# Deeper row buffers, a reordered product and an earlier convolution in a two-layer diffusion backbone

## The chip, the cores and the metric

The kernel runs on one core of a Trainium2 chip. The metric is the time of one execution in microseconds (us) on the device. Below, PE is the matrix engine, DVE the vector engine, ACT the scalar engine, POOL the GpSimd engine, and SP the engine that issues most loads. DMA transfers of all of them share 16 DMA engines.

## The reference

Two layers over 512 latent tokens x and 256 context tokens, width 1024, all in float32. A layer is a set of token mixers and then a PEER expert network:

```python
p = xn @ wl                                   # one input projection, 10 blocks of 1024 columns
attn = attn_out_norm(blocked_diff_attn(q, k, v, lam))
conv = (b_gate * depthwise_conv(c_gate * h, conv_w)) @ conv_out_w
merged = g[0] * attn + g[1] * pool + g[2] * conv      # g = sigmoid of three blocks of p
h = h + mod[2] * (merged @ w_out)

q = (xc @ w_q).reshape(T, 8, 2, 128)          # PEER: 8 heads, two halves
s = einsum('thid,hikd->thik', q, sub_keys)    # 128 keys per half; top 16 of each, top 16 of their sums
u = u_emb[eidx]                               # 128 of 16384 experts per token
hid = gelu(einsum('td,thkd->thk', xc, u))
h = h + mod[5] * einsum('thk,thkd->td', gate * hid, v_emb[eidx])
```

The context runs through the first layer completely; in the second it gives only keys and values.

## The kernel before

Weights and activations are split into a high and a low float32r part (`split`, lines 91 to 94: ACT copies the high part, DVE subtracts it to get the low one), and each product is three matmuls (`mm3`, lines 96 to 100): high by high, low by high, high by low. A weight tile is loaded by SP, split by ACT, then by DVE, and only then can PE use its low part.

The PEER network is computed in two ways. *Gathered*: for 256 context tokens in layer 0 and the last 128 x tokens in layer 1, the chosen rows of `peer_u` and `peer_v` are fetched, 128 tokens by 1024 floats a time, by an indirect DMA that POOL issues (line 855), into a buffer named `row`; DVE multiplies each with the token (line 868) or adds it to a sum (line 878). That makes 256 fetches for each 128 tokens, 768 in all: 512 in layer 0, 256 in layer 1. *Dense*: for 512 x tokens in layer 0 and 384 in layer 1 all 16384 experts are computed. `hidden` (line 766) loads 128 tiles `uraw`, splits each into `uh` and `ul`, and forms 128 products `hid` of 24 matmuls. `values` (line 817) forms 128 products `dps` in each layer from `vraw` tiles (`vh`, `vl`), added by DVE into `acc` (lines 838, 840). In layer 1 the first 20 of 32 chunks have their hidden parts stored, and the last 12 alternate between `hidden` and `values` (lines 1134 to 1140).

The gathered work is written at a priority 40000 steps behind, so it is meant to fill gaps of the dense work that runs beside it. A scheduler simulates the whole program and writes a fixed order of instructions for every engine; each engine then executes its own list strictly in that order. So if DVE's next instruction is a row that has not landed, everything behind it on DVE waits, splits included.

In layer 0 the order of stages is: attention of both streams, the context's mixers (`"pcgo"`), x's pooling, then `ctx_ffn` (norm, `keys`, `pick`, and the start of the gathered work of 256 tokens), x's remaining mixers (`mixers`, letters: g attention's gate, c convolution, o convolution's output and `w_out`), x's dense network with its own keys, `hidden`, `values`. `mm` tiles of x's mixers are taken from a pool of 3 PSUM banks (line 972), of which a core has 8. `hss` and `hrb` are the small matmuls of attention's gate (lines 492, 502, 503); `rsc` are the scores of `keys`; `gps` builds the gates of the dense experts.

Of the kernel before, what the change touches and what calls it, by code (L numbers as in the profile page):

```python
# [21 lines left out]
F32 = mybir.dt.float32  # L22
# [8 lines left out]
PSUM = bass.MemoryType.PSUM  # L31

P = 128
D = 1024
KT = D // P
# [34 lines left out]
class Net:  # L70
# [695 lines left out]
    def hidden(self, l, y, up, uq, cs, ahead, keep=False):  # L766

        nc, a = self.nc, self.a
        tiles = []
        for c in cs:  # L770
            if l:
                ge = up.tile([P, 4, y.n], F32, name="ge", bufs=1 + self.EC)
                tiles.append(ge)
            for e in range(4):
                with self.prio(-ahead):
                    raw = up.tile([P, KT, P], F32, name="uraw", bufs=3)
                    nc.sync.dma_start(raw.rearrange("p k e -> p (k e)"), a["uT"][l, 4 * c + e])
                    uh = up.tile([P, KT, P], F32R, name="uh", bufs=2)
                    ul = up.tile([P, KT, P], F32R, name="ul", bufs=2)
                    self.split(uh, ul, raw)  # L780
                hid = uq.tile([P, y.n], F32, name="hid", bufs=3)
                for k in range(KT):
                    self.mm3(hid, uh[:, k], ul[:, k], y.h[:, k], y.l[:, k], k == 0, k == KT - 1)
                with self.prio(-ahead):
                    g = ge[:, e] if l else up.tile([P, y.n], F32, name="ge", bufs=4)
                    nc.scalar.activation(g, hid, AF.Gelu_apprx_tanh)
                    if not l:
                        nc.scalar.dma_start(self.hidd[c][:, e * y.n:(e + 1) * y.n], g)
            if l and not keep:
                with self.prio(-ahead):  # L790
                    nc.scalar.dma_start(self.hidd[c][:, :4 * y.n], ge.rearrange("p e t -> p (e t)"))
        return tiles
# [56 lines left out]
    def gathered(self, l, tiles, gp, gq, nat, late):  # L849

        nc, a = self.nc, self.a

        def fetch(t, idx, s):
            r = gp.tile([P, D], F32, tag="row", name="row", bufs=3)
            nc.gpsimd.indirect_dma_start(out=r, out_offset=None, in_=a[t],  # L855
                                         in_offset=bass.IndirectOffsetOnAxis(ap=idx[:, s:s + 1], axis=0))
            return r

        for row, idx, g, hsrc, i, dst in tiles:
            with self.prio(late):  # L860
                x = gp.tile([P, D], F32, name="gx", bufs=1)
                nc.sync.dma_start(x, nat[row:row + P, :])
                acc = gp.tile([P, D], F32, name="gacc", bufs=1)
                for h in range(8):
                    hid = gp.tile([P, 16], F32, name="ghid", bufs=2)
                    for k in range(16):
                        r = fetch("peer_u", idx, h * 16 + k)
                        nc.vector.scalar_tensor_tensor(out=r, in0=r, scalar=1.0, in1=x, op0=OP.mult, op1=OP.mult,  # L868
                                                       accum_out=hid[:, k:k + 1])
                    w = gp.tile([P, 16], F32, name="gw", bufs=2)  # L870
                    nc.scalar.activation(w, hid, AF.Gelu_apprx_tanh)
                    nc.vector.tensor_tensor(w, w, g[:, h * 16:h * 16 + 16], op=OP.mult)
                    for k in range(16):
                        r = fetch("peer_v", idx, h * 16 + k)
                        if h == 0 and k == 0:
                            nc.vector.tensor_scalar(acc, r, w[:, k:k + 1], None, op0=OP.mult)
                        else:
                            nc.vector.scalar_tensor_tensor(acc, r, w[:, k:k + 1], acc, op0=OP.mult, op1=OP.add)  # L878
            res = gp.tile([P, KT, P], F32, tag="row", name="gres", bufs=3)
            nc.sync.dma_start(res, hsrc.rearrange("(k p) t -> p k t", p=P))  # L880
            tr = gq.tile([P, 4, P], F32, tag="gtr", name="gtr", bufs=1)
            for k in range(KT):
                nc.tensor.transpose(tr[:, k % 4], acc[:, k * P:(k + 1) * P], self.ident)
                nc.vector.scalar_tensor_tensor(res[:, k], tr[:, k % 4], self.modT[l][:, 40 + k, i:i + 1], res[:, k], op0=OP.mult, op1=OP.add)
            nc.sync.dma_start(dst.rearrange("(k p) t -> p k t", p=P), res)
# [10 lines left out]
    def run(self):  # L896
        nc, tc, a = self.nc, self.tc, self.a
        dt = lambda name, shape=(D, NT): tc.dram_tile(list(shape), F32, name=name)
        L = range(DEPTH)
        self.pd, self.od, self.md = [[dt(f"{n}{l}") for l in L] for n in ("pd", "od", "md")]  # L900
        self.qd, self.kd = [[dt(f"{n}{l}", (NH, P, 2, NT)) for l in L] for n in ("qd", "kd")]
        self.ld = [dt(f"ld{l}", (NH, P, NT)) for l in L]
        self.vd = [dt(f"vd{l}", (2, NH, P, NT)) for l in L]
        self.hmid = [dt(f"hmid{l}") for l in L]
        self.hout = dt("hout")
        self.natd = [dt("natd0", (NC, D)), dt("natd1", (P, D))]
        self.gd = dt("gd", (NX // 32, P, P * 32))
        self.hidd = dt("hidd", (32, P, 4 * NX))
        self.EC, self.stored = 2, 20
        X, Cx = Stream(0, NX, 0), Stream(NX, NC, 1)  # L910
        with ExitStack() as root:
            self.consts(self.pool(root, "consts"))
            ges = eh = h = None
            for l in L:
                ges, eh, h = self.trunk(l, X, Cx, ges, eh, h)
                ges, eh, h = self.ffn(l, ges, eh, h)
            eh.close()
            ges.close()
# [8 lines left out]
    def trunk(self, l, X, Cx, ges, eh, h):  # L927
# [6 lines left out]
        with ExitStack() as es, ExitStack() as ea, ExitStack() as ec:  # L934
            self.wpool, self.wbufs = self.pool(e3, f"wp{l}"), 3
            xp = self.parts(e3, f"xn{l}", X)
# [25 lines left out]
            if l == 0:  # L962
                self.attend(l, ea, [(Cx, XT, CT), (X, 0, TT)], "right")
                with ExitStack() as e2:
                    hc = self.mixers(l, Cx, self.pool(e2, "fc", 2, PSUM), cp, "pcgo")
                with ExitStack() as e2, self.prio(4000):
                    self.pooling(l, [X], self.pool(e2, "fp", 2, PSUM))
                ea.close()
                ges = self.ctx_ffn(l, hc)
                ec.close()  # L970
                with ExitStack() as e2:
                    hm = self.mixers(l, X, self.pool(e2, f"fl{l}", 3, PSUM), xp, "gco")
            else:
                ec.close()
                self.attend(l, ea, [(X, 0, TT)], "right")
                with ExitStack() as e2:
                    hm = self.mixers(l, X, self.pool(e2, f"fl{l}", 2, PSUM), xp, "pck|go", ea)
# [146 lines left out]
    def experts(self, l, y, up, uq, eu, e2):  # L1124


        n, EC, S = y.n, self.EC, self.stored
        with ExitStack() as es:
            self.hidden(l, y, up, uq, range(S), 12000)
            acc = self.pool(es, f"acc{l}").tile([P, KT, n], F32, name="acc")  # L1130
            va, vq = self.pool(es, f"va{l}"), self.pool(es, f"vq{l}", 1, PSUM)
            with ExitStack() as ev:
                vb = self.pool(ev, f"vb{l}")
                for c in range(S, 32 + EC, EC):
                    if c < 32:
                        ge = self.hidden(l, y, up, uq, range(c, c + EC), 0, True)
                    if c > S:
                        cs = range(c - EC, c)
                        self.values(l, n, cs, self.weigh(l, n, va, cs, had), lambda dq: (vb, 3, vb, EC + 2), vq, acc, c == S + EC)
                    had = ge  # L1140
                eu.close()
                e2.close()
            vb = self.pool(es, f"vc{l}", side="right")
            for c in range(0, S, EC):
                cs = range(c, c + EC)
                self.values(l, n, cs, self.weigh(l, n, va, cs), lambda dq: (vb, 3, vb, EC + 2), vq, acc, False,
                            vb if c == S - EC else None)
# [73 lines left out]
```

## Time and profile before

| | |
|---|---|
| median of 3 runs | 5116.54 us (5113.34 to 5140.52) |
| the profiled execution | 5126.48 us, its span 5124.7 us |
| PE, DVE busy in the span | 95%, 77% |
| ACT, POOL busy | 39%, 23% |
| mean granted PE clock | 0.975 of 2.4 GHz |
| DMA, mean over the span | 250 GB/s |

A busy PE is not a PE at its peak: its matmuls overlap. How dense they are is seen from their count in a stretch. "Idle before" an instruction is the idle time of its engine just before it, with what ended it. The stretches used below are cut at work that can be found again in any order: the first row fetch (991 us), the first split of `uraw` in layer 0 (1350), the first `acc` (2323) and the 57th (2621), the end of layer 0 (3006), in layer 1 shortly before the first fetch (3966) and the 57th `acc` (4833).

### The profile page before, as it was taken

The page shows a single profiled execution, that of the slowest core. Times are in us where ns is not written, and L with a number is a line of the kernel's source. Part 1 is how long each engine was busy: PE and PEld are TensorE (multiplying, and loading weights), DVE is VectorE, ACT ScalarE, POOL GpSimd, SP SyncE. Part 2 cuts the span into 40 slices and gives each one's busy share as a digit, 9 for nine tenths or more (in the row PEclk, how much of TensorE's full clock was granted, in tenths as well). Part 3 has the DMA queues.
Part 4 walks back from the last instruction along what each step waited for, and adds up shares of the span by engine and source line. Part 5 has one row for each costly group of instructions (what it writes and reads, how often), then busy time and mean ns, then how long its engine had stood idle before and what let it go on. Part 6 is the DMA issues. An engine that isn't in the chain of part 4 may idle for free.

```text
span 5124.7 us, 74008 instructions
## 1 busy us (share of the span) xinstructions
PE 4846.5 (95%) x27373; PEld 4187.1 (82%) x27373; DVE 3946.3 (77%) x7996; ACT 1984.5 (39%) x2970; POOL 1199.9 (23%) x1060
## 2 busy tenths in 40 slices
PE   8999999798799999989999999999999999899999
PEld 5689787576588788768888879888679889899999
DVE  5468785977799998568888766777459999787885
ACT  4346665222233344323222334555334344332333
POOL 0012000144433343243334100100000433244320
PEclk9999999899899999999999999999899999999999
DMA  8668554488888888999999734543355888988995
GB/s 308 239 201 237 179 169 129 145 271 276 281 302 270 297 300 323 323 315 320 342 335 337 261 114 161 175 135 118 120 169 173 282 297 329 319 313 292 335 330 177
DMA packets 509419, 1280.77 MB, mean 250 GB/s; under 512 B 42880, under 2 KB 225024, under 8 KB 500736
## 3 DMA queue, kind: packets, MB, share of 16 engines
q1 hardware_dynamic: 302816, 669.35, 38.7%
q0 software_dynamic: 132352, 449.90, 26.1%
q10 hardware_dynamic: 73888, 156.79, 8.2%
q8 instruction: 215, 3.52, 0.3%
q14 instruction: 148, 1.21, 0.1%
HBM read 1098.13 MB, written 177.73 MB: 249 GB/s over the span
## 4 chain that ended last, share of the span: by engine, by line
PE 47%; DMA 14%; issue 11%; DVE 9%; POOL 3%; ACT 1%; POOLq 0%; DVEq 0%; ACTq 0%; SPq 0%
DMA row<-peer_v,ix 8%; PE dps L100 6%; PE dps L99 6%; PE dps L98 6%; DMA row<-peer_u,ix 5%; PE mm L98 4%; PE mm L100 4%; PE mm L99 4%; PE hid L100 4%; PE hid L98 4%; PE hid L99 3%; POOL row L855 3%; DVE gacc L878 2%; PE gps L760 1%; PE qk L100 1%
## 5 line engine op out<-in xcount | busy, mean ns | idle before, releaser
L100 PE MATMUL hid<-yh,ul 128*128 128x512 f32 (+1 forms) x2048 | 760.8, 373 | 55.3 <-DVE ul L94 54.9
L855 POOL DMA_INDIRECT row<-peer_v,ix x384 | 586.7, 1528 | 876.9 <-DVE gacc L878 537.4
L98 PE MATMUL hid<-yh,uh 128*128 128x512 f32 (+1 forms) x2048 | 758.3, 371 | 21.0 <-ACT yh L286 13.1
L855 POOL DMA_INDIRECT row<-peer_u,ix x384 | 503.5, 1311 | 1113.7 <-DVE row L868 614.3
L99 PE MATMUL hid<-yl,uh 128*128 128x512 f32 (+1 forms) x2048 | 755.9, 369 | 3.6 <-DVE yl L287 3.6
L100 PE MATMUL dps<-wh,vl 128*128 128x512 f32 (+1 forms) x2048 | 740.9, 364 | 11.8 <-DVE vl L94 11.8
L99 PE MATMUL dps<-wl,vh 128*128 128x512 f32 (+1 forms) x2048 | 741.1, 364 | 7.0 <-DVE wl L94 7.0
L98 PE MATMUL dps<-wh,vh 128*128 128x512 f32 (+1 forms) x2048 | 735.3, 364 | 8.9 <-ACT vh L93 8.9
L98 PE MATMUL mm<-hi,whi 128*128 128x512 f32 (+1 forms) x1856 | 665.5, 359 | 19.6 <-ACT rg L481 6.0
L100 PE MATMUL mm<-hi,wlo 128*128 128x512 f32 (+1 forms) x1856 | 658.6, 357 | 25.3 <-DVE wlo L94 25.0
L99 PE MATMUL mm<-lo,whi 128*128 128x512 f32 (+1 forms) x1856 | 659.8, 356 | 1.7 <-DVE lo L94 1.7
L878 DVE SCALAR_TENSOR_TENSOR gacc<-row,gw,gacc 128x1024 f32<-128x1024 f32 x381 | 488.2, 1281 | 166.9 <-DMA row<-peer_v,ix 165.4
L868 DVE SCALAR_TENSOR_TENSOR row<-row,gx 128x1024 f32<-128x1024 f32 x384 | 466.9, 1222 | 168.5 <-DMA row<-peer_u,ix 167.9
L94 DVE TENSOR_TENSOR wlo<-wraw,whi 128x1024 fp32r<-128x1024 f32 (+1 forms) x356 | 428.1, 1204 | 178.5 <-ACT whi L93 175.7
L93 ACT ACTIVATE uh<-uraw 128x1024 fp32r<-128x1024 f32 x256 | 271.3, 1060 | 689.5 <-PE hid L99 657.4
L93 ACT ACTIVATE whi<-wraw 128x1024 fp32r<-128x1024 f32 (+1 forms) x356 | 369.9, 1043 | 385.3 <-PE mm L99 270.1
L93 ACT ACTIVATE vh<-vraw 128x1024 fp32r<-128x1024 f32 x256 | 270.1, 1057 | 633.6 <-PE dps L99 387.9
L100 PEld LDWEIGHTS hid<-yh,ul 128*128 128x128 f32 x2048 | 391.2, 191 | 107.4 <-DVE ul L94 69.3
L98 PEld LDWEIGHTS hid<-yh,uh 128*128 128x128 f32 x2048 | 392.1, 192 | 63.6 <-ACT yh L286 14.7
L100 PEld LDWEIGHTS dps<-wh,vl 128*128 128x128 f32 x2048 | 386.3, 189 | 53.2 <-DVE vl L94 12.7
L99 PEld LDWEIGHTS hid<-yl,uh 128*128 128x128 f32 x2048 | 391.4, 191 | 44.7 <-DVE yl L287 5.0
L98 PEld LDWEIGHTS dps<-wh,vh 128*128 128x128 f32 x2048 | 386.6, 189 | 49.9 <-ACT vh L93 9.7
(337 smaller groups left out, 9481.1 us busy)
## 6 DMA issues: line engine op xcount, KB each, us to landing
uraw<-uT SPq DMA_DIRECT2D x256, 512.0 KB
vraw<-v SPq DMA_DIRECT2D x256, 512.0 KB
wraw<-w_in SPq DMA_DIRECT2D x216, 512.0 KB
gd<-gst ACTq DMA_DIRECT2D x28, 2048.0 KB
mw<-w_mod SPq DMA_DIRECT2D x96, 512.0 KB
wraw<-wq SPq DMA_DIRECT2D x80, 512.0 KB
hidd<-ge ACTq DMA_DIRECT2D x128, 256.0 KB
G<-gd SPq DMA_DIRECT2D x32, 1024.0 KB
```

The costliest lines, as they stand in the source:

```text
L93: self.nc.scalar.activation(hi, src, AF.Copy)
L94: self.nc.vector.tensor_tensor(lo, src, hi.bitcast(F32), op=OP.subtract)
L98: mm(ps, lh, rh, start=start, stop=False)
L99: mm(ps, lh, rl, start=False, stop=False)
L100: mm(ps, ll, rh, start=False, stop=stop)
L760: nc.tensor.matmul(ps[:, t], A[:, a_, :, t_], B[x][:, a_, :, t_], start=x == 0, stop=x == 1)
L855: nc.gpsimd.indirect_dma_start(out=r, out_offset=None, in_=a[t], in_offset=bass.IndirectOffsetOnAxis(ap=idx[:, s:s + 1], axis=0))
L868: nc.vector.scalar_tensor_tensor(out=r, in0=r, scalar=1.0, in1=x, op0=OP.mult, op1=OP.mult, accum_out=hid[:, k:k + 1])
L878: nc.vector.scalar_tensor_tensor(acc, r, w[:, k:k + 1], acc, op0=OP.mult, op1=OP.add)
```

## The change

Five edits, of which four are of one line:

- `hidden` issues for a tile first the 16 matmuls that need only the high part `uh`, then the 8 that need `ul`. The count is the same.
- `row` buffers: 6 in layer 0 and 5 in layer 1 (`self.rows`), where there were 3.
- x's mixers in layer 0 run the convolution (c) before attention's gate (g), and their pool has 6 PSUM banks, where there were 3.
- In layer 1's alternating part the buffers for split `v` tiles are EC + 1 = 3, where there were 4.

```diff
                 hid = uq.tile([P, y.n], F32, name="hid", bufs=3)
+                mm = nc.tensor.matmul
                 for k in range(KT):
-                    self.mm3(hid, uh[:, k], ul[:, k], y.h[:, k], y.l[:, k], k == 0, k == KT - 1)
+                    mm(hid, uh[:, k], y.h[:, k], start=k == 0, stop=False)
+                    mm(hid, uh[:, k], y.l[:, k], start=False, stop=False)
+                for k in range(KT):
+                    mm(hid, ul[:, k], y.h[:, k], start=False, stop=k == KT - 1)
...
-            r = gp.tile([P, D], F32, tag="row", name="row", bufs=3)
+            r = gp.tile([P, D], F32, tag="row", name="row", bufs=self.rows[l])
...
-            res = gp.tile([P, KT, P], F32, tag="row", name="gres", bufs=3)
+            res = gp.tile([P, KT, P], F32, tag="row", name="gres", bufs=self.rows[l])
...
-        self.EC, self.stored = 2, 20
+        self.EC, self.stored, self.rows = 2, 20, (6, 5)
...
-                    hm = self.mixers(l, X, self.pool(e2, f"fl{l}", 3, PSUM), xp, "gco")
+                    hm = self.mixers(l, X, self.pool(e2, f"fl{l}", 6, PSUM), xp, "cgo")
...
-                        self.values(l, n, cs, self.weigh(l, n, va, cs, had), lambda dq: (vb, 3, vb, EC + 2), vq, acc, c == S + EC)
+                        self.values(l, n, cs, self.weigh(l, n, va, cs, had), lambda dq: (vb, 3, vb, EC + 1), vq, acc, c == S + EC)
```

Since the scheduler sees other buffers, the written order of all engines differs from the context's expert network in layer 0 on. PE, at the end of the context's `keys` in layer 0, before:

```order
L660 MATMUL rsc<-keys,rq 128x128 x6
L492 MATMUL hss<-osq,sel 8x512 x8
L502 MATMUL hrb<-hrh,selb 128x512 x2
L98 MATMUL mm<-hi,whi 128x512
L99 MATMUL mm<-lo,whi 128x512
```

PE at the same place after (`mm` here is the convolution):

```order
L660 MATMUL rsc<-keys,rq 128x128 x5
L98 MATMUL mm<-hi,whi 128x512
L99 MATMUL mm<-lo,whi 128x512
L100 MATMUL mm<-hi,wlo 128x512
L98 MATMUL mm<-hi,whi 128x512
```

and PE further on, where `hss` now stands:

```order
L99 MATMUL mm<-lo,whi 128x512
L100 MATMUL mm<-hi,wlo 128x512
L492 MATMUL hss<-osq,sel 8x512 x8
L502 MATMUL hrb<-hrh,selb 128x512 x2
L98 MATMUL mm<-hi,whi 128x512
```

Where `hss` followed the keys directly, 672 `mm` matmuls now stand between (the convolution's 576 and 96 of the gates). The 96 of the gates stood before `keys`, between the steps of the context's norm, where none stands now.

DVE, in `values` of layer 0 between the 36th and the 40th `acc`, before:

```order
L840 TENSOR_TENSOR acc<-dps,acc 128x512
L878 SCALAR_TENSOR_TENSOR gacc<-row,gw,gacc 128x1024 x2
L94 TENSOR_TENSOR vl<-vraw,vh 128x1024
L878 SCALAR_TENSOR_TENSOR gacc<-row,gw,gacc 128x1024
L840 TENSOR_TENSOR acc<-dps,acc 128x512
L94 TENSOR_TENSOR vl<-vraw,vh 128x1024
L878 SCALAR_TENSOR_TENSOR gacc<-row,gw,gacc 128x1024 x2
```

and after (lines are 4 higher):

```order
L94 TENSOR_TENSOR vl<-vraw,vh 128x1024
L872 SCALAR_TENSOR_TENSOR row,ghid<-row,gx 128x1024
L94 TENSOR_TENSOR vl<-vraw,vh 128x1024
L872 SCALAR_TENSOR_TENSOR row,ghid<-row,gx 128x1024 x3
L844 TENSOR_TENSOR acc<-dps,acc 128x512
L94 TENSOR_TENSOR vl<-vraw,vh 128x1024
L872 SCALAR_TENSOR_TENSOR row,ghid<-row,gx 128x1024
```

Rows stand closer together, and the last of layer 0 stands ahead of the 57th `acc`, where it stood ahead of the 105th; in layer 1 ahead of the 57th, where it stood ahead of the 97th. Counted on DVE's list:

| rows on DVE's list | before | after |
|---|---|---|
| first fetch to first `ul` of layer 0 | 119 | 129 |
| to the first `acc` | 242 | 290 |
| to the 57th `acc` | 79 | 93 |
| to the end of layer 0 | 72 | 0 |
| layer 1, to its 57th `acc` | 222 | 256 |
| to the end | 34 | 0 |

## Rows read from the trace of the kernel before

**Rows 1.** The page: engines; DMA queues (packets, MB, share of 16 engines).

```profile
PE 4846.5 (95%) x27373; PEld 4187.1 (82%) x27373; DVE 3946.3 (77%) x7996; ACT 1984.5 (39%) x2970; POOL 1199.9 (23%) x1060
...
q1 hardware_dynamic: 302816, 669.35, 38.7%
q0 software_dynamic: 132352, 449.90, 26.1%
q10 hardware_dynamic: 73888, 156.79, 8.2%
```

**Rows 2.** The page's groups: xcount | busy us, mean ns | idle before, releaser.

```profile
L100 PE MATMUL hid<-yh,ul 128*128 128x512 f32 (+1 forms) x2048 | 760.8, 373 | 55.3 <-DVE ul L94 54.9
...
L878 DVE SCALAR_TENSOR_TENSOR gacc<-row,gw,gacc 128x1024 f32<-128x1024 f32 x381 | 488.2, 1281 | 166.9 <-DMA row<-peer_v,ix 165.4
L868 DVE SCALAR_TENSOR_TENSOR row<-row,gx 128x1024 f32<-128x1024 f32 x384 | 466.9, 1222 | 168.5 <-DMA row<-peer_u,ix 167.9
```

**Rows 3.** Windows: us, busy of PE, PEld, DVE, ACT, POOL; clock, DMA share, GB/s.

```profile
848.50:889.00 40.50, 32.66 (x132) 24.88 (x131) 14.87 (x30) 22.23 (x45) 0.00 (x0) 0.83 0.38 126
889.00:956.00 67.00, 59.60 (x448) 55.06 (x447) 55.74 (x264) 22.76 (x35) 2.36 (x10) 0.98 0.51 172
956.00:991.00 35.00, 19.02 (x33) 6.81 (x33) 35.00 (x208) 10.76 (x15) 0.00 (x0) 0.65 0.00 0
991.00:1350.00 359.00, 312.24 (x1258) 243.00 (x1257) 268.34 (x352) 86.61 (x108) 157.07 (x139) 0.94 0.82 276
1350.00:2323.00 973.00, 919.51 (x5111) 764.46 (x5110) 819.24 (x1778) 344.16 (x513) 356.65 (x243) 0.97 0.87 303
2323.00:2621.00 298.00, 298.00 (x1317) 246.82 (x1316) 260.01 (x345) 90.34 (x115) 106.85 (x79) 1.00 0.95 332
2621.00:3006.00 385.00, 380.23 (x1675) 312.42 (x1674) 290.67 (x383) 105.62 (x133) 100.35 (x70) 1.00 0.80 277
...
3966.00:4833.00 867.00, 811.10 (x5052) 788.02 (x5051) 742.01 (x1284) 317.80 (x482) 331.70 (x226) 0.98 0.87 307
4833.00:5125.00 292.00, 287.67 (x1662) 287.05 (x1660) 220.87 (x331) 97.62 (x131) 44.04 (x31) 1.00 0.77 266
```

**Rows 4.** Windows of short, dense stretches, columns as in Rows 3.

```profile
2432.00:2560.00 128.00, 128.00 (x567) 106.01 (x566) 110.78 (x149) 36.28 (x46) 46.17 (x36) 1.00 0.97 337
2550.00:2600.00 50.00, 50.00 (x222) 41.44 (x221) 45.31 (x67) 15.12 (x19) 17.89 (x16) 1.00 1.00 354
```

**Rows 5.** Windows of tile row: DVE busy, POOL busy; clock, share, GB/s.

```profile
1350.00:2323.00 973.00, 302.33 (x363) 355.11 (x242) 0.97 0.87 303
```

**Rows 6.** Who waited for whom, PE, 956 to 1350 us: total, times, longest.

```profile
PE mm L100 <- DVE wlo L94: 24.5, 14, 4.2
PE hrb L502 <- ACT hrh L93: 9.2, 1, 9.2
PE nps L275 <- DVE hmid L631: 8.7, 1, 8.7
PE hss L492 <- ACT osq L491: 6.8, 1, 6.8
```

**Rows 7.** The same, 1350 to 2323 us.

```profile
PE hid L100 <- DVE ul L94: 16.8, 12, 4.0
PE dps L100 <- DVE vl L94: 11.0, 1, 11.0
PE hid L98 <- ACT yh L286: 7.4, 1, 7.4
```

**Rows 8.** The same, 3966 to 4833 us.

```profile
PE hid L100 <- DVE ul L94: 38.1, 21, 5.8
PE dps L98 <- ACT vh L93: 7.1, 1, 7.1
PE dps L100 <- DVE vl L94: 0.7, 1, 0.7
```

**Rows 9.** Timeline of PE from 956 us: start, us, what, idle before.

```profile
956.05 5.61 PE L492 MATMUL hss<-osq,sel 128*8 128x512 f32 x8
968.45 6.23 PE L492 MATMUL hss<-osq,sel 128*8 128x512 f32 x8 [6.79 <-ACT osq L491]
983.87 1.22 PE L502 MATMUL hrb<-hrh,selb 8*128 8x512 f32 x2 [9.20 <-ACT hrh L93]
```

## The prediction

> **What bounds the kernel now.** I read the page first. PE is busy 95% of the span [rows 1], but its largest group stands idle for 55.3 us before it, nearly all of it for the low part `ul` that DVE makes, and DVE itself idles 168 and 165 us for fetched rows [rows 2]. So there is a chain: row, DVE, split, PE. Next the windows, cut where rows and dense work can be compared. There the reader is to see three columns: matmuls in a stretch, DVE's busy time and the DMA rate. From 2323 to 2621 us PE has no gap (298 of 298), the clock is 1.00 and DMA moves 332 GB/s at a share of 0.95; in the three others with fetches PE is busy 312 of 359, 919 of 973 and 811 of 867 us, and DMA moves 276, 303 and 307 GB/s [rows 3]. At its densest PE issues 567 matmuls in 128 us, one in 226 ns [rows 4]. Last the waits of PE in each of these stretches: 24.5 us for weight splits, 16.8 and 38.1 us for `ul` [rows 6 to 8]. PE is the bound, it loses some 150 us of named and unnamed gaps in the four stretches (47 + 54 + 0 + 56, busy against length), and the transfers are near a bound of their own.
>
> **What the change does to the four stretches.** With 6 and 5 buffers a fetch is issued five and four rows ahead of the one that DVE works on, instead of two. A row costs DVE some 1.25 us [rows 2], and other work lies between rows, so the landing has more than double the time. The written order uses that: it puts rows closer together, and all of them earlier (the counts stand in the section on the change). A row is 128 x 1024 x 4 bytes = 0.524 MB. So what each stretch must move is its rate by its length, plus the rows that enter it:
>
> 991 to 1350: 0.276 x 359 = 99.1 MB, and 10 rows, 5.2 MB: 104.3.
> 1350 to 2323: 0.303 x 973 = 294.8 MB, and 48 rows, 25.2 MB: 320.0.
> 2323 to 2621: 0.332 x 298 = 98.9 MB, and 14 rows, 7.3 MB: 106.3.
> 3966 to 4833: 0.307 x 867 = 266.2 MB, and 34 rows, 17.8 MB: 284.0 [rows 3].
>
> That is 759.0 MB in 2497 us now (304 GB/s), and 814.6 MB after. To keep the time, DMA has to move 326 GB/s on average. PE would let the four stretches shrink by about 150 us; DVE would too, since 48 rows add 60 us to its 819 in the second stretch and 34 add 43 to 742 in the last, both under the new lengths. POOL spends 355 us on 242 fetches there, 1.5 us each [rows 5]; 290 of them fit well into 950 us. So the rate of the transfers decides. What can it be? By the page, the three queues moved 1276.0 MB in 73.0% of the span, which is 341 GB/s while the engines are busy [rows 1]. A dense stretch of 128 us has 337 at a share of 0.97, one of 50 us has 354 at 1.00 [rows 4], and the third stretch 332 over 298 us [rows 3]. I take the middle of 332 and 337, 334.5, because these are long and have the same mixture of fetches and loads, and because deeper fetches leave the queue of rows less often empty. 814.6 / 0.3345 = 2435 us: 62 us less than now. By stretch: -47, -16, +20, -18. The third gets longer: it is full already and has 14 rows more. Ends: at 332 it is -43, at 341 it is -108.
>
> The Trainium skill's page "DMA: Bandwidth & Descriptors", under "Where 436 GB/s comes from", says that between HBM and SBUF the HBM side binds at about 358 GB/s, while its page "HBM Reference", under "Specifications (TRN2)", has a core that streams alone at about 425. The trace's 354 at a share of 1.00 [rows 4] speaks for the first. By 358 the four stretches would take 814.6 / 0.358 = 2275 us, an estimate from that page, and by 425 transfers would bind nowhere here; in both PE would be the bound again, which is the third rival below.
>
> **The reordered product.** It removes nothing and adds nothing: 24 matmuls either way. `ul` is wanted 16 matmuls x 226 ns = 3.6 us after the tile's start instead of 0.5, so 3.2 us later (2.4 where a matmul has 384 columns, by 4833 to 5125, where 1662 take 292 us [rows 3]). Its waits, 16.8 and 38.1 us, have longest pieces of 4.0 and 5.8 and means of 1.4 and 1.8 us [rows 7, 8], so most of them would go, some 40 of 55 us. I don't add this to the sum: where transfers bind, PE then waits for a later thing. It is what lets PE follow DMA's pace. Without it, these 40 us would be at risk.
>
> **The convolution ahead of the gate.** Now PE stands at 956 us before `hss`, waits 6.8 us for it and 9.2 us for `hrb`, and runs at a clock of 0.65 of full speed, while DVE is busy all 35 us with `pick` [rows 3, 6, 9]. Afterwards the convolution's matmuls fill that hole: six banks hold 6 tiles of 24 matmuls, 33 us of PE work that can wait for DVE. Against it: the 96 matmuls that stood in the context's norm (96 x 0.226 = 21.7 of 40.5 us [rows 3]) are gone from there, so the norm keeps its bare 18.8 us, and everything behind it starts some 20 us sooner; the same 21.7 us come back later. That is nothing, give or take 3. And `hss` to `hrb` is met again behind the convolution, with nothing between: 9.2 us [rows 9], and 6 more, since DVE's list now has five rows of 1.25 us between the steps of that little chain. 16 us dead before, 15 after. What is gained is that loads run (none now from 956 to 991, DMA share 0.00 [rows 3]) and that the clock stays up; a part of this is already in the -47 of the first stretch, which transfers set. I count nothing on its own; bounds -10 (the clock: 35 us at 0.65 cost 12) and +12 (if DVE's rows hold the small chain for twice as long).
>
> **The third buffer for `v`, and what is left.** In the alternating part a split tile has one spare buffer instead of two. Now PE waits 7.1 us once for `vh` and 0.7 for `vl` [rows 8]. Below: nothing. Above: 24 quarter passes (6 of 4) by one DVE split of 1.2 us, 29 us. I take 4, near the row. From 2621 to 3006 and from 4833 on no row is left after the change, but PE is busy 380 of 385 and 288 of 292 us already [rows 3]: -4 and -2.
>
> **Sum.** -62 + 0 + 4 - 6 = -64 us on the profiled execution, 5126.5 (its span, and 1.8 us around it) to 5062. That execution was 9.9 us above the median of the runs. Taken from the median: 5116.5 - 64 = 5052.
>
> **Rivals.** (1) *Slower: rows that are late hold DVE.* The order ties each row to earlier dense work than before; if DMA serves less than the break-even 326 GB/s, DVE stands at a row, and the `wlo`, `ul` or `vl` behind it on its list is late for PE. Place: the second and third stretch, where PE now waits only 16.8 us or not at all. At 318 GB/s: 814.6 / 0.318 = 2562, +65, with the other terms +63: 5180. For it: the three stretches with gaps have never gone over 307, and DVE idles 333 us for rows in all [rows 2]. Against it: the third stretch holds 332 with no PE gap at all. (2) *Nothing to measure.* DMA reaches 322 to 330, or it reaches 334 and the third `v` buffer costs its 29 us: the time lands within 0.5% of 5116.5, say 5105. For it: 326 lies between the two groups of rates that the trace shows. (3) *PE is the bound again.* If fetches that lie deep in the queue let DMA run at its 354 of the short window, the four stretches need 2301 us for transfers, 196 less, and PE's 150 us of gaps go first: 5116.5 - 150 = 4966. For it: the 354 stands beside a PE busy 50 of 50 us. Against it: it is held for 50 us only, and the start of each stage has waits on norms (8.7, 7.4 and 11.0 us [rows 6, 7]) that no row buffer removes.
>
> **How the numbers follow.** Forecast 0.60, rival 1 0.11, rival 2 0.18, rival 3 0.11. The forecast's own range is 332 to 341 GB/s with the side terms: 5005 to 5085. 0.5%, 25.6 us, is about what a measurement of this kernel tells from no change; all of the forecast and rival 3 lie under 5091. Faster 0.71, same 0.18, slower 0.11. For 8 in 10 the range runs into rival 3 down to 4985, and over rival 2 into rival 1 up to 5125.
>
> **What would show it.** Windows: 330 GB/s or more in the stretches to the 57th `acc` of either layer, with the last row of layer 0 at about 2550 us. Waits: DVE's for rows well under half of 333 us; PE's for `ul` under 20 of 55; the hole behind `keys` filled with `mm`, and a wait of 9 to 16 us at `hrb` some 150 us later. Wrong if the rate stays near 304 and DVE's row waits don't fall; if the third stretch grows by far more than 20 us; or if `ul` waits stay, which would make DVE's work and not its waits the cause.

## The result and the profile after

The changed kernel takes 5038.02 us (median of 4, 5031.36 to 5042.78). Runs of the kernel before beside it had 5114.94, a ratio of 0.9837 with a 95% interval of 0.9804 to 0.9871: 77 us less between the medians. The profiled execution has a span of 5034.5 us, 90.2 less than before. The profiled execution before took 11.5 us more than the median beside it and the one after 1.8 less, so lengths read from the two profiles differ by some 13 us more than the medians.

The page of the kernel after: engines, DMA queues (to be held against [rows 1]).

```profile
PE 4812.7 (96%) x27373; PEld 4178.7 (83%) x27373; DVE 3948.3 (78%) x7996; ACT 2015.1 (40%) x2970; POOL 1210.8 (24%) x1060
...
q1 hardware_dynamic: 302816, 669.35, 39.3%
q0 software_dynamic: 132352, 449.90, 25.4%
```

Its groups (busy us, mean ns, idle before and what ended most of it), against [rows 2]:

```profile
L98 PE MATMUL dps<-wh,vh 128*128 128x512 f32 (+1 forms) x2048 | 737.4, 365 | 43.4 <-ACT vh L93 34.2
...
L882 DVE SCALAR_TENSOR_TENSOR gacc<-row,gw,gacc 128x1024 f32<-128x1024 f32 x381 | 486.9, 1278 | 21.5 <-DMA row<-peer_v,ix 19.0
...
L872 DVE SCALAR_TENSOR_TENSOR row<-row,gx 128x1024 f32<-128x1024 f32 x384 | 461.7, 1216 | 15.0 <-DMA row<-peer_u,ix 14.8
L787 PE MATMUL hid<-yh,ul 128*128 128x512 f32 (+1 forms) x2048 | 467.9, 366 | 0.0
```

DVE's waits for rows fell from 333 to 34 us and PE's for `ul` from 54.9 to 0.0. One wait grew, PE's for `vh`, to 34.2 us. Before it was 8.9:

```profile
L98 PE MATMUL dps<-wh,vh 128*128 128x512 f32 (+1 forms) x2048 | 735.3, 364 | 8.9 <-ACT vh L93 8.9
```

Windows of the kernel after, cut at the same work as [rows 3] (busy of PE, PEld, DVE, ACT, POOL; clock, DMA share, GB/s):

```profile
868.00:936.00 68.00, 61.13 (x454) 57.56 (x454) 52.85 (x231) 28.75 (x53) 1.93 (x1) 0.89 0.40 138
936.00:987.00 51.00, 47.07 (x197) 38.22 (x196) 50.98 (x261) 13.75 (x19) 0.26 (x4) 0.93 0.18 61
987.00:1301.00 314.00, 292.82 (x1209) 227.55 (x1207) 276.35 (x363) 97.38 (x123) 193.43 (x153) 0.97 0.92 338
1301.00:2240.00 939.00, 906.34 (x5108) 758.56 (x5108) 870.98 (x1853) 357.76 (x512) 428.48 (x292) 0.98 0.93 340
2240.00:2552.00 312.00, 300.63 (x1297) 243.95 (x1297) 277.98 (x368) 87.72 (x113) 111.32 (x87) 0.99 0.95 339
2552.00:2933.00 381.00, 381.00 (x1684) 315.47 (x1683) 210.12 (x273) 106.91 (x132) 0.00 (x0) 1.00 0.57 183
3891.00:4738.00 847.00, 794.29 (x5032) 778.56 (x5032) 778.90 (x1322) 327.03 (x481) 374.21 (x257) 0.97 0.93 334
4738.00:5034.00 296.00, 292.43 (x1690) 291.81 (x1688) 186.20 (x284) 98.45 (x131) 0.00 (x0) 1.00 0.62 205
```

I call the four stretches with rows A (first fetch to first `ul`), B (to the first `acc`), C (to the 57th) and E (layer 1, to its 57th). Their change: A 359 to 314 (-45), B 973 to 939 (-34), C 298 to 312 (+14), E 867 to 847 (-20). All four together took 85 us less. The rest, some 5 us, is small change ahead of A, between the layers and behind C and E. In the last window ahead of the first fetch PE was busy 19 of 35 us at a clock of 0.65; now (936 to 987) it is busy 47 of 51 us at 0.93.

Who waited for whom on PE after, first from 936 to 1301 us (total, times, longest; [rows 6]):

```profile
PE hrb L502 <- ACT hrh L93: 7.7, 1, 7.7
PE mm L100 <- DVE wlo L94: 4.5, 4, 1.8
PE hss L492 <- ACT osq L491: 4.0, 1, 4.0
```

Then from 1301 to 2240 us ([rows 7]):

```profile
PE hid L784 <- ACT yh L286: 14.1, 1, 14.1
PE dps L98 <- ACT wh L93: 6.6, 2, 4.8
PE hid L784 <- ACT uh L93: 6.6, 3, 2.8
PE hid L785 <- DVE yl L287: 6.5, 2, 3.5
```

These sum to 33.8 us, about all of PE's idle time in B (939 - 906.3 is 32.7). Most of them stand where a product begins: 20.6 us at 1311 to 1325, where the norm's output `yh`, `yl` is late for `hidden`, and 6.6 at 2208 to 2225, where the first weights are late for `values`. The 6.6 for `uh` stand at 2085 to 2123, in 100 us in which DMA moves 384 GB/s (2045 to 2145). And from 3891 to 4738 us ([rows 8]):

```profile
PE dps L98 <- ACT vh L93: 30.5, 1, 30.5
PE hid L784 <- ACT uh L93: 9.0, 6, 3.8
PE gps L760 <- DVE gB L752: 8.4, 6, 2.8
```

### The profile page after: what moved, and what is told of

Its sections match the earlier page's. It is cut to its first block, busy times and chain, and to the rows that moved or that the text cites. A ratio compares the mean times of both kernels' runs of the same rounds, so it can differ in the third digit from the quotient of the medians.

```text
span 5034.5 us, 73915 instructions
## 1 busy us (share of the span) xinstructions
PE 4812.7 (96%) x27373; PEld 4178.7 (83%) x27373; DVE 3948.3 (78%) x7996; ACT 2015.1 (40%) x2970; POOL 1210.8 (24%) x1060
## 4 chain that ended last, share of the span: by engine, by line
PE 66%; issue 8%; DVE 6%; DMA 3%; ACT 2%; POOL 1%; SPq 0%; ACTq 0%; DVEq 0%; POOLq 0%
PE dps L100 7%; PE hid L784 7%; PE dps L98 7%; PE dps L99 7%; PE hid L785 7%; PE hid L787 7%; PE mm L98 4%; PE mm L99 4%; PE mm L100 4%; PE gps L760 2%; PE qk L100 1%; PE qk L98 1%; PE qk L99 1%; DVE row L872 1%; DMA vraw<-v 1%
## 5 line engine op out<-in xcount | busy, mean ns | idle before, releaser
L98 PE MATMUL dps<-wh,vh 128*128 128x512 f32 (+1 forms) x2048 | 737.4, 365 | 43.4 <-ACT vh L93 34.2
L787 PE MATMUL hid<-yh,ul 128*128 128x512 f32 (+1 forms) x2048 | 467.9, 366 | 0.0
L99 PEld LDWEIGHTS dps<-wl,vh 128*128 128x128 f32 x2048 | 386.2, 189 | 43.6 <-DVE wl L94 3.4
```

Source lines behind the costliest of these rows:

```text
L98: mm(ps, lh, rh, start=start, stop=False)
L99: mm(ps, lh, rl, start=False, stop=False)
L787: mm(hid, ul[:, k], y.h[:, k], start=False, stop=k == KT - 1)
```

## Experiments

Each kernel was timed beside the kernel before on one chip, so ratios are compared, not times of different chips. Theory T is the prediction's: the transfers set the pace of A, B, C and E. This table is put together from all profiles: lengths of the stretches between the same work in us (E is the sum of its two halves), DVE's waits for rows and PE's waits for `ul` from the groups. The profiled execution of prod_only took 17 us more than the median of its runs, so its lengths are long.

```
kernel       ratio   95% interval    A    B    C    E   row waits  ul waits
before       1                       360  973  298  867   333       55
after        0.9837  0.9804-0.9871   314  939  313  848    34        0
rows_only    0.9886  0.9868-0.9903   306  953  312  870    41       24
prod_only    1.0005  0.9991-1.0018   364  990  298  869   345       21
no_prod      0.9884  0.9866-0.9903   310  959  317  856    53       25
no_conv      0.9841  0.9822-0.9861   309  945  319  848    42        4
half_uv      0.9805  0.9790-0.9820   313  950  295  859    54        2
light_dve    0.9754  0.9736-0.9771   302  936  311  843    47        8
s22          0.9774  0.9760-0.9787   315  938  313  823    28        0
s24          0.9776  0.9762-0.9791   311  942  310  827    30        0
before_half  1.0119  1.0100-1.0138   357 1002  329  874   329       63
s22_r75      0.9818  0.9799-0.9837   322  951  321  816    26        0
s22_r44      0.9748  0.9729-0.9767   320  937  295  823    84        1
light_pe     0.9669  0.9635-0.9703   315  848  316  852    43        5
```

### One part alone, or all but one

**rows_only**: before, with

```diff
-name="row", bufs=3        (and gres)
+name="row", bufs=self.rows[l]        # (6, 5)
-lambda dq: (vb, 3, vb, EC + 2)
+lambda dq: (vb, 3, vb, EC + 1)
```

> The kernel before with the 6 and 5 row buffers alone (and the third v buffer in place of the fourth, for the room). Theory T (the transfers set the pace of the stretches with rows, and deeper fetches let them run at 335 to 340 GB/s): nearly the whole gain is here, 5114.9 - 60 to 75, 5040 to 5055; DVE waits under 60 us for rows instead of 333. Rival P (PE's waits for the low part ul were the cost, and the reordered product is what pays): 5085 to 5115, with ul waits of 40 us or more. If T holds but PE needs the new order to follow, up to 40 us less than T: 5080 to 5095.

**prod_only**: before, with the two new loops over k in `hidden` and nothing else.

> The kernel before with the reordered product alone. T: ul waits go (55 to under 10 us) but DVE still waits some 330 us for rows and PE for other things behind them, so 5095 to 5115. P: 5070 to 5080, the 40 us of ul waits gone for good.

**no_prod**: after, with the one old loop.

> The changed kernel with the three matmuls of a step of the product in the old order. T with transfers as the only pace: 5038 to 5045. T with the product as what lets PE follow (as the prediction put it, 40 us at risk): 5060 to 5080, ul waits back at 40 us or more. P: 5080 to 5100.

**no_conv**: after, with

```diff
-self.pool(e2, f"fl{l}", 6, PSUM), xp, "cgo")
+self.pool(e2, f"fl{l}", 3, PSUM), xp, "gco")
```

> The changed kernel with attention's gate ahead of the convolution again, and 3 banks. The prediction counted this edit at nothing, between -10 and +12: 5026 to 5050 is within it. Rival G (the filled hole at the keys is a gain of its own, 15 to 35 us): 5053 to 5073.

Measured: 5068.5, 5129.3, 5065.4 and 5046.9 us. The rows bring 1.1 of the 1.6%; the time of rows_only lies between T's two ranges. The reordered product brings nothing by itself (the kernel before had 5126.8 beside it), though it takes `ul` waits from 55 to 21 us, where T said under 10: DVE's row waits stay at 345, and PE waits for other things behind them. Beside the deeper buffers it brings half a per cent. The changed kernel and no_prod differ by it (0.9837 against 0.9884, intervals that just overlap), and so do no_conv and rows_only, timed on one chip (0.9841 against 0.9886, intervals apart). It lies in B (953 and 959 without it, 945 and 939 with it) and in E (870 and 856, against 848). So P falls, and T with the product as what lets PE follow holds in sign; its 40 us came out as some 24, about the 25 us of `ul` waits that no_prod has. The convolution's place brings nothing that can be measured (0.9841 against 0.9837): with the gate first, A is 5 us shorter, what stands ahead of A is 9 longer, and the hole at the keys is back. G falls.

### Are the transfers the pace?

**half_uv**: after, with half of each dense tile loaded and used twice (half of the weights are left out), the same for `vraw`:

```diff
-nc.sync.dma_start(raw..., a["uT"][l, 4 * c + e])
-self.split(uh, ul, raw)
+nc.sync.dma_start(raw[:, :KT // 2]..., a["uT"][l, 4 * c + e][:, :D // 2])
+rb = raw[:, None, :KT // 2].to_broadcast([P, 2, KT // 2, P])
+self.split(uh..., ul..., rb)
```

> The changed kernel, but of every dense u and v tile only one half is loaded and used twice (half of the dense weights are left out); ACT, DVE and PE do the same work. That takes 128 x 0.262 = 33.5 MB from the stretch from the first ul to the first acc, 15 MB from the one to the 57th acc, some 44 MB from layer 1's. Theory T (transfers set the pace): these shrink until PE has no gaps left (PE is busy 906 of 939, 301 of 312 and 794 of 847 us), 60 to 95 us in all: 4943 to 4978. Rival V (DVE's work sets it: busy 198 of 199, 197 of 200, 195 of 200 us from 1301 to 1900): under 15 us: 5023 to 5040.

**light_dve**: after, both row operations on the first half of the columns; the other half is left out.

```diff
-scalar_tensor_tensor(out=r, in0=r, scalar=1.0, in1=x, ...)
-scalar_tensor_tensor(acc, r, w[:, k:k + 1], acc, ...)
+scalar_tensor_tensor(out=r[:, :D // 2], in0=r[:, :D // 2], scalar=1.0, in1=x[:, :D // 2], ...)
+scalar_tensor_tensor(acc[:, :D // 2], r[:, :D // 2], w[:, k:k + 1], acc[:, :D // 2], ...)
```

> The changed kernel, but DVE multiplies and adds only the first half of each fetched row (the other half is left out); every byte is still fetched. DVE saves some 0.53 us on each of 768 rows, 150 us between the first ul and the first acc of layer 0. T: no more than 12 us either way, 5026 to 5050. V: the same stretches shrink by 40 to 90 us, 4950 to 4998.

**light_pe**: after, with a sixth of the matmuls of `hidden` in layer 0 left out:

```diff
-mm(hid, uh[:, k], y.l[:, k], start=False, stop=False)
+if l or k < KT // 2:
+    mm(hid, uh[:, k], y.l[:, k], start=False, stop=False)
```

> The changed kernel with 4 of the 24 matmuls of each hid tile of layer 0 left out (half of the products with the token's low part). PE has 128 x 4 x 0.226 = 116 us less to do between the first ul and the first acc; the written order puts 241 rows there instead of 290. Theory P (behind the deeper buffers PE is the pace there, not transfers, not DVE): that stretch falls from 939 to 823 to 850 us, the one behind it grows by 5 to 20 us for its 11 rows more, in all 4935 to 4965. Rival (DVE's work or the transfers are nearly as tight, so that PE then waits for ul): 890 us or more there, ul waits of 30 us or more, 4990 to 5030.

Measured: 5033.1, 5004.7 and 4955.3 us. The first is in V's range, the second between T's and V's, the third in P's. Windows of half_uv, the stretches B, C and E:

```profile
1297.00:2247.00 950.00, 911.34 (x5106) 762.19 (x5107) 887.00 (x1880) 357.22 (x510) 444.09 (x305) 0.97 0.87 307
2247.00:2541.00 294.00, 294.00 (x1302) 243.04 (x1301) 264.74 (x349) 88.18 (x113) 111.42 (x75) 1.00 0.86 292
3878.00:4737.00 859.00, 799.42 (x5038) 781.52 (x5038) 783.75 (x1339) 329.21 (x481) 423.87 (x257) 0.96 0.82 279
```

B and E did not get shorter (950 and 859 against 939 and 848): DMA simply moved less in the same time, 307 instead of 340 and 279 instead of 334 GB/s. T is refuted there. The kernel after itself has 200 us inside B in which DMA moves more than the mean of any of the four stretches, beside a PE that is hardly ever idle:

```profile
1900.00:2100.00 200.00, 198.37 (x1244) 162.31 (x1243) 177.89 (x247) 83.00 (x129) 88.64 (x60) 1.00 0.96 367
```

C did get shorter: 313 to 295, and PE has no gap left. The written order also has 80 rows there instead of 93, so the 18 us may not all be from the loads.

Window of light_dve, stretch B:

```profile
1282.00:2218.00 936.00, 904.70 (x5097) 757.89 (x5098) 733.99 (x1883) 355.17 (x511) 384.91 (x307) 0.98 0.95 350
```

DVE has 137 us less work, and B is 3 us shorter. So V is refuted in B too. The kernel as a whole is 32 us of span shorter, of which A has 12, the time ahead of A 6, E 5 and the rest small pieces; neither theory had put it there. In C, DVE has a quarter of its time free, and PE has gaps all the same where the fetches lie close (72 of them in the first 212 us, a DMA share of 1.01):

```profile
2218.00:2430.00 212.00, 205.66 (x888) 166.47 (x887) 159.27 (x255) 61.45 (x79) 86.22 (x72) 0.99 1.01 364
```

A share above 1 says that the packet times of this account overlap; shares near 1 are to be read with that margin. So in C it is not DVE's work that PE waits for. In B PE is left, and light_pe bears it out. Its A, B and C:

```profile
987.00:1304.00 317.00, 291.83 (x1206) 226.72 (x1204) 277.62 (x367) 97.92 (x124) 196.91 (x153) 0.96 0.93 338
1304.00:2142.00 838.00, 789.38 (x4554) 658.24 (x4555) 799.97 (x1766) 348.50 (x505) 384.72 (x240) 0.97 0.94 345
2142.00:2460.00 318.00, 303.69 (x1304) 244.64 (x1303) 288.17 (x384) 86.64 (x112) 144.77 (x103) 0.99 1.00 358
```

With 116 us of matmuls out, B falls by 91, to 848 us between the anchors (the window is cut 10 us ahead of the first `acc`). Its order has 241 rows there instead of 290, 25.7 MB less, so this run alone does not part PE from the transfers; half_uv does, which took 33.5 MB of loads out of B, put 13 rows (6.8 MB) more into it, and did not make it shorter. So P, which in this run means PE as the pace, holds in B: its matmuls, and its waits at the starts of the products. C, with 104 rows in the written order, has a DMA share of 1.00 and 14 us of PE gaps.

### What made the rows late before

**before_half**: the kernel before with the edit of half_uv.

> The kernel before (3 row buffers), loading only one half of every dense u and v tile and using it twice (half of the dense weights are left out). What made rows late there? Theory L (depth: only two fetches are under way ahead, however free the transfers are): DVE's waits for rows stay over 250 of 333 us, ratio 0.995 to 1.003. Theory T' (in this kernel the transfers did set the pace, by what the dense loads take from the fetches): waits under 150 us, ratio 0.985 to 0.993, that is 35 to 75 us.

Measured: 5186.7 us, ratio 1.0119: slower, which no theory had. On the waits L is right: 329 us, as with all bytes; its 0.995 to 1.003 for the time is not. Groups of before_half:

```profile
L879 DVE SCALAR_TENSOR_TENSOR gacc<-row,gw,gacc 128x1024 f32<-128x1024 f32 x381 | 489.3, 1284 | 161.9 <-DMA row<-peer_v,ix 160.1
L869 DVE SCALAR_TENSOR_TENSOR row<-row,gx 128x1024 f32<-128x1024 f32 x384 | 468.0, 1223 | 170.9 <-DMA row<-peer_u,ix 169.2
```

B takes 1002 and C 329 us, with `ul` waits of 63. A likely cause, which no run isolates, is its written order: 275 rows in B and 100 in C where the kernel before has 242 and 79. How a row comes to be late is seen in the kernel before, where buffers turn around. POOL's timeline (start, us, what, idle before):

```profile
2248.79 1.86 POOL L855 DMA_INDIRECT row<-peer_v,ix  x1 [3.83 <-DVE gacc L878]
...
2256.88 1.67 POOL L855 DMA_INDIRECT row<-peer_v,ix  x1 [2.91 <-DVE gacc L878]
```

and DVE's there:

```profile
2247.23 2.61 DVE L878 SCALAR_TENSOR_TENSOR gacc<-row,gw,gacc 128x1024 f32<-128x1024 f32 x2 [3.08 <-DMA row<-peer_v,ix]
...
2255.32 1.29 DVE L878 SCALAR_TENSOR_TENSOR gacc<-row,gw,gacc 128x1024 f32<-128x1024 f32 x1 [2.56 <-DMA row<-peer_v,ix]
...
2263.65 1.28 DVE L878 SCALAR_TENSOR_TENSOR gacc<-row,gw,gacc 128x1024 f32<-128x1024 f32 x1 [1.82 <-DMA row<-peer_v,ix]
```

DVE gives a buffer back at 2248.5 and POOL refills it from 2248.79; with three buffers this is the third row on, and DVE gets it at 2255.32, 6.5 us later. It frees it, POOL starts at 2256.88, and DVE has the row at 2263.65. That is 8.3 us a turn and three rows a turn, while DVE's share of a turn is 3 x 1.28. Over all rows between 1310 and 2240 us for which DVE waited, the median from POOL's start to DVE's, worked out from the trace, is about 8 us (some 60 rows); in before_half it is about 7 (some 60 rows). With half of the dense bytes away it is 1 us less. The load fell by less than that sounds (303 to 276 GB/s in B, since more rows stand there), so this alone is a weak test. What settles it is rows_only: every byte is fetched, and with 6 and 5 buffers the row waits are 41 us instead of 333 while DMA in B moves 338 GB/s. It is a delay, and depth covers it.

The Trainium skill's page "DMA: Bandwidth & Descriptors", under "Anatomy of one DMA — SWDGE (gpsimd) path", fits a DMA issued by POOL with 2.0 us plus bytes over 436 GB/s. By that a row would take 3.2 us, an estimate from that page. The trace does not agree: 6.5 to 8 us from POOL's start, for an indirect fetch beside dense loads.

### The new wait in layer 1

PE's 30.5 us for `vh` begin at 4322.7. PE after:

```profile
4321.05 1.65 PE L760 MATMUL gps<-gB,gA 128*128 128x128 f16 x14 [0.20 <-DVE gB L753]
4353.23 0.69 PE L98 MATMUL dps<-wh,vh 128*128 128x384 f32 x1 [30.53 <-ACT vh L93]
```

ACT and SP's queue, the same time:

```profile
4323.37 0.33 ACTq L763 DMA_DIRECT2D gd<-gst  x1
```

```profile
4332.94 2.43 SPq L805 DMA_DIRECT2D G<-gd  x2
4335.47 5.96 SPq L830 DMA_DIRECT2D vraw<-v  x3
```

The last gates go out to memory at 4323.4, the first `G` can be read back only at 4332.9, and the `vraw` loads stand behind it on SP's list. SP's own wait for it, from 4300 to 4370:

```profile
SPq L805 <- DMA gd<-gst: 27.1, 1, 27.1
```

In the written order before, 95 `hid` matmuls stood between the last gate matmul (`gps`) and the first `dps`; after, none. With 22 or 24 stored chunks there are 120 and 144.

**s22**, **s24**: after, with

```diff
-self.EC, self.stored, self.rows = 2, 20, (6, 5)
+self.EC, self.stored, self.rows = 2, 22, (6, 5)        # s24: 24
```

> The changed kernel with 22 of 32 chunks of layer 1 stored instead of 20, so that dense products stand between the last gate matmuls and the first dps. Theory H (the 30.5 us wait for vh and the slow clock beside it are 46 us lost): 4990 to 5010. Rival T (transfers went on at 358 GB/s in that hole, so the time comes back later, as DVE or PE waiting for loads): 5025 to 5045.

> The same with 24 chunks stored: 2 chunks more are written out and read back, 3.1 MB and so 9 us of transfers at 340 GB/s. H: 4990 to 5020. T: 5030 to 5055.

Measured: 5016.2 and 5019.7 us. Against after's ratio that is 0.6% less in both, and the intervals don't overlap. E falls from 848 to 823, and 8 of these 25 us come back behind it, where 18 rows are left. H holds, with about half of its 46 us: s24 is in its range, s22 6 us above it. The two windows, after and s22:

```profile
4300.00:4366.00 66.00, 25.80 (x161) 22.80 (x160) 52.64 (x71) 17.59 (x31) 30.42 (x19) 0.59 0.99 358
```

```profile
4301.00:4368.00 67.00, 51.92 (x337) 50.34 (x336) 52.15 (x64) 27.87 (x43) 22.25 (x17) 0.90 0.98 353
```

The same transfers, 358 and 353 GB/s, and twice the matmuls. Still, s22 has a wait of 13.3 us for `vh`.


### How deep is deep enough

**s22_r75**, **s22_r44**: s22 with (7, 5) and (4, 4) row buffers.

> 22 chunks stored and 7 row buffers in layer 0. In the written order 76 rows stand between the first and the 57th acc instead of 93, and 8 and 9 more in the two stretches ahead. If transfers bind only that stretch: 17 x 0.524 = 8.9 MB less, at 338 GB/s 26 us less, down to PE's floor of 295 to 299 us, so 13 to 18 less than 313, the stretches ahead unchanged: 4997 to 5005 where s22 has 5016. If they bind the stretches ahead too, these take 17 x 0.524 / 0.34 = 26 us more: 5016 to 5030.

> 22 chunks stored and 4 row buffers in both layers. How deep is deep enough? In the order 81 rows stand in the stretch to the 57th acc and 48 behind it, where transfers have room. Theory L in steps (each buffer takes its part): DVE waits for rows 120 to 220 us, 5030 to 5055. Rival (one buffer more is enough, and rows left for the end of layer 0 are free): waits under 60 us, 5000 to 5015.

Measured: 5037.6 and 5001.1 us. The first expectation failed: 5037.6 lies above both of its ranges. Stretch C of s22_r75, in two parts:

```profile
2258.00:2460.00 202.00, 189.70 (x801) 153.86 (x800) 189.04 (x246) 54.38 (x68) 97.08 (x71) 0.97 1.02 368
2460.00:2579.00 119.00, 117.77 (x523) 96.78 (x522) 74.61 (x101) 37.50 (x47) 0.00 (x0) 1.00 0.64 209
```

It has fewer rows there, as the order says, but all in the first 202 us: 71 fetches at a share of 1.02, and PE loses 12 us in that part. Then DMA has room, at a share of 0.64. B grew by 13 at the same 340 GB/s, in PE's waits late in it: 9.8 us for `uh` at 2135 and 11.4 for `wh` at 2247, where the kernel after has at most 2.8 and 4.8. What makes these longer no run explains. In s22_r44 the 81 rows lie over the whole of C:

```profile
2242.00:2537.00 295.00, 295.00 (x1303) 244.34 (x1302) 259.81 (x353) 89.81 (x115) 106.38 (x82) 1.00 0.97 343
```

343 GB/s, and no PE gap. Row waits are 84 us, more than the 60 that the rival gave and less than theory L's 120, and the time is the rival's: one buffer more does most of it. s22_r44 is faster than the changed kernel (0.9748 against 0.9837, the intervals lie apart); from s22 it differs by no more than the intervals allow. The two runs differ in layer 1 too (5 buffers and 4); the lengths compared here, A, B and C, are layer 0's.

## Why the prediction was right, and where not

The time (5052 against 5038), the sign and three of the four lengths came out (-47, -16, +20, -18 against -45, -34, +14, -20). The reason given for them, the rate of the transfers, holds in C alone; it failed in B and E, and for A it is open. So the nearness in E is luck: the forecast held transfers for the pace there and did not see the hole. And the nearness of the whole is in part luck too: B fell by 18 more than forecast, and the -64 of the sum was -77 between the medians.

- **"So the rate of the transfers decides": failed in B and E, right in C.** The 338, 340 and 334 GB/s that came are above the break-even of 326 and beside the assumed 334.5. But a rate in a stretch is its bytes over its length, whatever sets the length: half_uv has nearly the same lengths at 307 and 279. Nor did the trace hold one rate that could be taken as the bound: at shares of 0.97 to 1.00 the windows of the two kernels show from 337 (before, 128 us) to 380 GB/s (after, 200 us), and no run shows what makes the difference. What set them before was DVE at rows with two fetches under way ahead of it and some 8 us to land; what sets B now is PE, by half_uv, light_dve and light_pe together. In C, where the share reaches 0.95, half_uv and s22_r44 take PE's gaps away, and the forecast +20 was +14. A was not settled: light_dve takes 12 us from it, 4 buffers with 317 instead of 338 GB/s add 5.
- **B was mis-sized (-16, measured -34)** for that reason: the working let the transfers hold B at 957 us, where PE is busy for 906 and waits 33 more, mostly at the starts of products.
- **The reordered product** was worked out rightly: nothing alone, and what lets PE follow. No `ul` wait is left (forecast under 20); without it the kernel takes some 24 us more, where 40 were said to be at risk.
- **The convolution at nothing** holds: 0.9841 without it. The hole is filled, and `hss` and `hrb` wait 4.0 and 7.7 us further on: together within the 9 to 16, `hrb` alone under it.
- **The third v buffer**, +4: PE waits 1.0 us for `vl` in E, as good as nothing. The wait for `vh` that looks like it comes from `G`; prod_only, with four v buffers, has it too (22.9 us).
- **Behind C and behind E**, -4 and -2: -4 and +4.
- **What the prediction missed**: the hole in layer 1. E's -20 is what is left behind it; s22 fills half.
- **Rivals.** 1 and 2 are out. Rival 3, PE the bound again, has the mechanism of B, and its own counter-argument (waits at the starts of products) is one reason why its 4966 was not reached; C's transfers and the hole are others that the windows show. What the prediction held against it, 354 GB/s "for 50 us only", was short: from 4817 to 4917 the kernel before moves 358 with PE busy all 100 us, and from 1946 to 2146 the kernel after 380.
- **The signs named did not tell the theories apart.** They came true: 334 GB/s and more, no fetch on POOL behind 2552, row waits a tenth, `ul` at 0. The windows of half_uv and light_pe were needed.

The 358 GB/s that the prediction took from the Trainium skill's page "DMA: Bandwidth & Descriptors", under "Where 436 GB/s comes from", are no ceiling in the trace: the kernel after moved 380 over 200 us at a share of 0.99 (1946 to 2146). So the reading that the 354 of the kernel before speaks for that page doesn't hold. The 425 of "HBM Reference", under "Specifications (TRN2)", no run shows over 40 us or more; the nearest here is 417, from 1946 to 1986 in the kernel after.

## What to carry to other kernels

A wait for a fetch is cured by more fetches under way if the fetch is a delay, and only by fewer bytes if it is a rate; the busy share of DMA does not tell which, but a run with more buffers and the same bytes does. A rate computed from a stretch confirms no bound: take the suspected load away and see if the stretch gets shorter. Deeper buffers also let a scheduler bunch fetches, so more depth than the delay needs can cost what it brought (here 7 buffers against 4 in layer 0).

## What was not expected of the hardware

A row's fetch of 0.524 MB, where DVE waited for it, took a median of about 8 us from POOL's start to DVE's use while DMA moved 303 GB/s in all, and about 7 at 276. And the kernel after moved 380 GB/s for 200 us beside a PE busy 193 of them, above the 354 that the prediction took from its densest window; the densest 200 us of the kernel before moved 347 (from 4762).

```profile
1946.00:2146.00 200.00, 193.45 (x1120) 157.85 (x1119) 164.27 (x213) 76.73 (x112) 87.70 (x62) 0.99 0.99 380
```
